# A hybrid encoder trunk on one core: half of branch C's gated product stays in on-chip memory, and the residual loads are queued behind the merge's loads

## The chip, the core and the metric

The kernel runs on one core of a Trainium2 chip. The metric is the device time of one execution, in microseconds (us). Five engines work side by side, each with its own queue of instructions that it starts in order: TensorE (PE, matmuls and transposes; its weight loads are listed as PEld), VectorE (DVE), ScalarE (ACT), GpSimd (POOL) and SyncE (SP). Here SP issues the loads of weights, and POOL issues most of the transfers of intermediate results. All transfers share 16 DMA engines. Tiles live in on-chip memory (SBUF) of 128 partitions; matmul results live in eight PSUM banks.

## The reference

The trunk has two layers over 512 positions of width 1024. Cut to what matters here:

```python
z = rms_norm(x, ln1[l]) @ w_in[l]
...
y_a = rms_norm(o_a, a_norm[l]) * silu(a_g)        # branch A: gated linear recurrence
y_b = spatial_gating(gelu(b_u), gelu(b_v), ...)   # branch B: gMLP
y_c = window_attention(qh, kh, vh, sink[l])       # branch C: windowed attention
gates = sigmoid(gz.reshape(bsz, s_len, 3, D_MODEL))
merged = (gates[:, :, 0] * (y_a @ w_br[l, 0])
          + gates[:, :, 1] * (y_b @ w_br[l, 1])
          + gates[:, :, 2] * (y_c @ w_br[l, 2]))
x = x + merged @ w_out[l]
x = x + square(relu(rms_norm(x, ln2[l]) @ w_up[l])) @ w_down[l]
```

All of it is in float32. The output is the final RMSNorm of x, 512 x 1024.

## The kernel before, in words

**Matmuls.** Each float32 product is made of three matmuls. An operand is split into a rounded high part and the rest: for weights ACT casts `wh <- wr` (L207) and DVE subtracts `wl <- wr,wh` (L208); for data the same is done at L262 and L263. A chunk of weights is 128 x 1024 (512 KB), loaded by SP (L187) into one of two raw buffers; there are three pairs of split buffers, so the cast for a later chunk waits until PE has let go of an earlier pair.

**The order of the work.** The program is written as one long sequence. A planner then simulates it with a model of its own of how long everything takes, and fixes the order on every engine's queue: an instruction that is ready in that simulation goes first, by priority. The order is therefore fixed before the kernel runs, and each engine keeps to it. Lines under `hp()` have raised priority. Semaphores and the reuse of buffers are handled by the same system, so a transfer into a buffer waits until the last reader of that buffer has finished.

**The merge of a layer.** Data is in feature order in some places and in token order in others. `proj_tok` (L254 to L256) computes a token-ordered product: four PSUM banks, one for each block of 128 tokens, 512 columns, so that a width of 1024 takes two halves (`fl` = 0 and 1). There are two groups of four banks; `proj_tok` is given one of them. The steps, for each layer, are these:

1. Branch B's gated product in feature order, `mg`, is stored to DRAM (`mgd`, L902) early.
2. The gates of branches C and A, in token order, have been stored to DRAM (`thd`) and are loaded back by `gates` (L1006) as tiles `th`.
3. Branch C: for each half, `gates`, `proj_tok` (tile `yC`), then for each token block `th <- th,yC` on DVE (L1053), a store of it to `mcd` by POOL (L1054).
4. The branch pool (`br`) ends, and the pool `Y2` (tags `yi`, `th`, `mg`) takes over its memory.
5. Branch A, for each half: `gates` (four loads `th`), four loads `mC <- mcd` (L1087), `proj_tok` (tile `yA`), then for each token block `th <- th,yA` (L1092) and the sum `mC <- mC,th` (L1093).
6. `turn_sum(fl)`: for each of four feature blocks, PE transposes the four sums into a bank (tile `mT`, L1072), POOL loads branch B's part, `mB <- mgd` (L1075), DVE adds, `mB <- mB,mT` (L1077), and the result is split into `mgh` and `mgl` (L262, L263). `turn_sum(0)` stands behind the first half in the program and uses two banks of the group that the first half has used. `turn_sum(1)` is called in the middle of the first half of the output projection.
7. The residual stream is loaded, eight tiles `xr` (L1102), from the input in layer 0 and from `xspill` in layer 1. The output projection `wo` (two halves of `proj_tok`, over eight feature blocks) follows, its first half in the banks that `turn_sum(0)` has used, and `xr <- wo,xr` (L1108) adds the residual.
8. A norm, transposes and the MLP (`up`, `dA`, `dB`, `dC`) follow.

A tile comes from `T(tag, name)`; a tag has a number of slots of 128 x 512 float32 (256 KB), listed in `SLOTS`. A tag named in `HOME` belongs to a pool that lives for a part of the layer; any other tag is permanent. The lines around step 5 are:

```python
for fl in range(2):
    th = gates("th", 1, fl)
    mc = []
    for t in range(4):
        m = T("mg", "mC")
        nc.gpsimd.dma_start(m, mcd[:, fl * 4 + t])
        mc.append(m)
    pts = proj_tok(ys, "yA", (l, "y", 0, fl), fl)
```

Of the kernel before, what the change touches and what calls it, by code (L numbers as in the profile page):

```python
# [6 lines left out]
F32 = mybir.dt.float32  # L7
# [3 lines left out]
ALU = mybir.AluOpType  # L11

P = 128
S = 512
# [46 lines left out]
def trunk(tc, xT, xt, ws, vec, fnb, bsb, snk, wst, rope, cmask, amask, ident, out):  # L61
    nc = tc.nc
# [3 lines left out]
    def pool(**kw):  # L66
        p = tc.tile_pool(**kw)
        pools.append(p)
        return p.__enter__()
# [6 lines left out]
    dram = pool(name="dram", bufs=1, space=bass.MemoryType.DRAM)  # L76

    SLOTS = {"x": 16, "l": 8, "l2": 4, "tv": 8, "rb": 1, "jk": 1,  # L80
             "xs": 16, "zt": 6,
             "yh": 8,
             "q": 2, "a": 3, "g": 2, "ch": 10,
             "yi": 16, "th": 8, "mg": 8,
             "h": 22}

    HOME = {t: p for p, ts in {"G": ("xs", "zt"), "Y1": ("yh",), "br": ("q", "a", "g", "ch"), "Y2": ("yi", "th", "mg"), "mlp": ("h",)}.items() for t in ts}
# [5 lines left out]
    def nm(s):  # L93
        ctr[0] += 1
        return f"{s}_{ctr[0]}"

    def T(tag, name, dt=F32):
        where = part[HOME[tag]] if tag in HOME else sb
        return where.tile([P, S], dt, tag=tag, bufs=SLOTS[tag], name=nm(name))

# [32 lines left out]
    def hp():  # L133

        return tc.high_priority() if boost[0] else contextlib.nullcontext()
# [104 lines left out]
    def proj_tok(xs, name, key, group, mid=None):  # L240

        pts = [PT(tag, name) for tag in GROUPS[group]]
        nk = len(xs)
        for i in range(nk // 2):
            if mid and i == nk // 4:
                mid()
            hi, lo = wload(*key, i)
            for k2 in range(2):
                k = 2 * i + k2
                c = slice(k2 * S, (k2 + 1) * S)  # L250
                for t in range(4):
                    tt = slice(t * P, (t + 1) * P)
                    xh, xl = xs[k][0][:, tt], xs[k][1][:, tt]
                    nc.tensor.matmul(pts[t], xh, hi[:, c], start=k == 0, stop=False)  # L254
                    nc.tensor.matmul(pts[t], xl, hi[:, c], start=False, stop=False)
                    nc.tensor.matmul(pts[t], xh, lo[:, c], start=False, stop=k == nk - 1)  # L256
        return pts

    def split(src, hi, lo, scale=None):

        if scale is None:
            nc.scalar.copy(hi, src)  # L262
            nc.vector.tensor_tensor(lo, src, hi.bitcast(F32), ALU.subtract)  # L263
        else:
            nc.scalar.activation(hi, src, AF.Copy, scale=scale)
            nc.vector.scalar_tensor_tensor(lo, src, scale, hi.bitcast(F32), ALU.mult, ALU.subtract)  # L266
# [39 lines left out]
    def norm_tok(which, l, xr, keep):  # L306

        n = Norm()
        n.xs, n.xf = [None] * KT, [None] * KT
        n.ss = SM("ss8", 8)  # L310

        def add(t, fl):
            j = T("jk", "jk")
            nc.scalar.activation(j, xr[t][fl], AF.Square, accum_out=n.ss[:, t * 2 + fl:t * 2 + fl + 1])

        def turn(fl, ts, bank="s"):

            w = len(ts) * P
            c0 = ts[0] * P
            for d in range(4 * fl, 4 * fl + 4):  # L320
                if n.xs[d] is None:
                    n.xs[d] = (T("x", "xh", F32R), T("x", "xl", F32R))
                    if keep:
                        n.xf[d] = Z() if d < 4 else T("l", "xf")
                pt = PT(bank, "xT")
                for i, t in enumerate(ts):
                    nc.tensor.transpose(pt[:, i * P:(i + 1) * P], xr[t][fl][:, (d % 4) * P:(d % 4 + 1) * P], id_t)
                src = pt[:, 0:w]
                parts = [x[:, c0:c0 + w] for x in n.xs[d]]
                if keep:  # L330
                    xf = n.xf[d][:, c0:c0 + w]
                    nc.scalar.activation(xf, src, AF.Copy, scale=ln_ap(which, l, d))
                    split(xf, *parts)
                else:
                    split(src, *parts, ln_ap(which, l, d))

        def end():
            s = SM("s4", 4)
            nc.vector.tensor_tensor(s, ap_of(n.ss, 0, [[2, 4]]), ap_of(n.ss, 1, [[2, 4]]), ALU.add)
            n.rc = rstd_c(s, D)  # L340

        n.add, n.turn, n.end = add, turn, end
        return n
# [345 lines left out]
    for i in range(8):  # L689
        t = T("tv", "xt")  # L690
# [5 lines left out]
    xsrc = xt  # L696
    xspill = dram.tile([P, 4, D], F32, name="xspill")
    thd = dram.tile([P, 8, D], F32, name="thd")
    mgd = dram.tile([P, KT, S], F32, name="mgd")
    mcd = dram.tile([P, 8, S], F32, name="mcd")  # L700

    for l in range(DEPTH):
        xs = n1.xs
# [176 lines left out]
        def y_split(ys, tag):  # L880
            res = []
            for y in ys:
                hi, lo = T(tag, "yh", F32R), T(tag, "yl", F32R)
                split(y, hi, lo)
                res.append((hi, lo))
            return res
# [19 lines left out]
        def gate_a():  # L906
            z = evac(proj(xs, "ag", l, "ag", len(sg)), "l2", "ag")
            th = T("jk", "th")
            nc.scalar.activation(th, z, AF.Tanh, scale=0.5)
            nc.vector.scalar_tensor_tensor(z, th, 1.0, z, ALU.add, ALU.mult)  # L910
            sg.append(z)
# [89 lines left out]
        def gates(tag, i, fl):  # L1001

            res = []
            for t in range(4):
                z = T(tag, "th")
                nc.gpsimd.dma_start(z, thd[:, i * 4 + t, fl * S:(fl + 1) * S])  # L1006
                res.append(z)
            return res
# [34 lines left out]
        with later(30000):  # L1043
            for h in range(4):
                gate_a()

            ys = y_split(yc, "yh")
            for fl in range(2):
                th = gates("ch", 0, fl)
                pts = proj_tok(ys, "yC", (l, "y", 2, fl), 0)  # L1050
                for t in range(4):
                    with hp():
                        nc.vector.scalar_tensor_tensor(th[t], th[t], 1.0, pts[t], ALU.add, ALU.mult)  # L1053
                    nc.gpsimd.dma_start(mcd[:, fl * 4 + t], th[t])  # L1054
        ys = []
        for h in range(4):
            nc.vector.scalar_tensor_tensor(oa[h], oa[h], 0.5, sg[h], ALU.mult, ALU.mult)
# [9 lines left out]
        def turn_sum(fl):  # L1067

            for d in range(4 * fl, 4 * fl + 4):
                pt = PT("s" if fl else "c", "mT")  # L1070
                for t in range(4):
                    nc.tensor.transpose(pt[:, t * P:(t + 1) * P], mcs[fl][t][:, (d % 4) * P:(d % 4 + 1) * P], id_t)  # L1072
                hi, lo = T("yi", "mgh", F32R), T("yi", "mgl", F32R)
                m = T("th", "mB")
                nc.gpsimd.dma_start(m, mgd[:, d])  # L1075
                with hp():
                    nc.vector.tensor_tensor(m, m, pt, ALU.add)  # L1077
                    split(m, hi, lo)
                ms[d] = (hi, lo)

        ms = [None] * KT
        for fl in range(2):
            th = gates("th", 1, fl)
            mc = []
            for t in range(4):
                m = T("mg", "mC")
                nc.gpsimd.dma_start(m, mcd[:, fl * 4 + t])  # L1087
                mc.append(m)
            pts = proj_tok(ys, "yA", (l, "y", 0, fl), fl)
            for t in range(4):  # L1090
                with hp():
                    nc.vector.scalar_tensor_tensor(th[t], th[t], 1.0, pts[t], ALU.add, ALU.mult)  # L1092
                    nc.vector.tensor_tensor(mc[t], mc[t], th[t], ALU.add)  # L1093
            mcs.append(mc)
            if fl == 0:
                turn_sum(0)


        xr = [[T("l", "xr"), T("l", "xr")] for _ in range(4)]
        for fl in range(2):  # L1100
            for t in range(4):
                nc.gpsimd.dma_start(xr[t][fl], xsrc[:, t, fl * S:(fl + 1) * S])  # L1102
        n2 = norm_tok("ln2", l, xr, False)
        for fl in range(2):
            pts = proj_tok(ms, "wo", (l, "wo", fl), fl, None if fl else lambda: turn_sum(1))
# [88 lines left out]
        xsrc = xspill  # L1194
# [121 lines left out]
```

## Time and profile before

| | |
|---|---|
| median of three runs | 1730.86 us (1730.69 to 1731.39) |
| profiled execution, span | 1729.5 us |
| mean granted TensorE clock | 0.996 |
| busy: PE, PEld | 97%, 81% |
| busy: DVE, ACT, POOL | 75%, 59%, 8% |
| transfers | 200.04 MB, of which POOL's queue 43.40 MB |
| stores to `mcd`, loads from it | 16 and 16, of 256 KB each |
| loads `xr` | 8 in each layer, of 256 KB each |
| merge of layer 0, of layer 1 | about 455 to 506 us, about 1313 to 1364 us |

The profile is one execution on the chip. Rows of a timeline give the start, the duration, the engine, the line of the kernel, the operation, the tile written and the tiles read, the count of merged instructions, and in brackets the idle time of the engine before it with what ended that idle time. Matmuls are pipelined, so the time that one costs is read from start to start. "Busy" of PE counts pipelined matmuls, and is an average over stages with different limits.

### The profile page before, as it was taken

How to read it: one execution, taken by the hardware profiler on the slowest of the kernel's cores; microseconds unless marked ns; L12 is line 12 of the kernel's file. 1: busy time of each engine (PE TensorE's matmuls, PEld its weight loads, DVE VectorE, ACT ScalarE, POOL GpSimd, SP SyncE). 2: the span in 40 equal slices, each digit the busy share in tenths (PEclk: the TensorE clock that was granted, in tenths of full speed). 3: DMA queues.
4: the chain of work that ended last, by engine and by line, in shares of the span. 5: the costliest groups of instructions: out<-in, count | busy, mean ns of one | idle time of the engine just before them, and what ended most of it. 6: DMA issues, size and time to landing. Idle time of an engine off the chain costs nothing.

```text
span 1729.5 us, 21976 instructions
## 1 busy us (share of the span) xinstructions
PE 1685.3 (97%) x8024; PEld 1405.0 (81%) x8024; DVE 1297.1 (75%) x2009; ACT 1017.1 (59%) x1715; POOL 146.1 (8%) x215
## 2 busy tenths in 40 slices
PE   8999999999999999999999999999999999999997
PEld 7888878887877888888888787888877878888886
DVE  7996977687566668686889869876776567686867
ACT  7665567677335555545665754877772355545454
POOL 0011200000310000000010112000004000000001
PEclk9999999999999999999999999999999999999999
DMA  8342232231545332233423422322317353232311
GB/s 331 98 146 92 83 104 81 72 104 55 203 187 182 98 110 98 98 98 98 134 92 126 147 93 71 104 79 75 111 48 273 130 182 98 98 98 97 119 65 49
DMA packets 58283, 200.04 MB, mean 116 GB/s; under 512 B 7904, under 2 KB 8288, under 8 KB 58176
## 3 DMA queue, kind: packets, MB, share of 16 engines
q1 hardware_dynamic: 44640, 154.72, 26.6%
q0 software_dynamic: 13248, 43.40, 6.7%
q8 instruction: 63, 1.03, 0.3%
q10 hardware_dynamic: 288, 0.52, 0.1%
q14 instruction: 44, 0.36, 0.1%
HBM read 177.64 MB, written 20.97 MB: 115 GB/s over the span
## 4 chain that ended last, share of the span: by engine, by line
PE 43%; issue 20%; DVE 4%; ACT 2%; POOL 0%; POOLq 0%; ACTq 0%; DVEq 0%
PE up L213 3%; PE up L212 3%; PE up L214 3%; PE dA L418 2%; PE dA L420 2%; PE dA L419 2%; PE at L558 1%; PE gA L418 1%; PE gz L214 1%; PE gz L213 1%; PE gz L212 1%; PE dC L418 1%; PE dC L420 1%; PE dC L419 1%; PE gA L420 1%
## 5 line engine op out<-in xcount | busy, mean ns | idle before, releaser
L207 ACT CAST wh<-wq 128x1024 fp32r<-128x1024 f32 x201 | 211.4, 1052 | 208.2 <-PE up L213 49.3
L208 DVE TENSOR_TENSOR wl<-wq,wh 128x1024 fp32r<-128x1024 f32 x201 | 245.1, 1222 | 117.1 <-ACT wh L207 116.1
L208 DVE TENSOR_TENSOR wl<-wr,wh 128x1024 fp32r<-128x1024 f32 x166 | 203.9, 1228 | 148.0 <-ACT wh L207 147.6
L207 ACT CAST wh<-wr 128x1024 fp32r<-128x1024 f32 x166 | 174.0, 1049 | 214.6 <-PE up L213 67.3
L212 PE MATMUL up<-xh,wh 128*128 128x512 f32 x512 | 199.2, 390 | 1.9 <-ACT u L1171 1.9
L213 PE MATMUL up<-xl,wh 128*128 128x512 f32 x512 | 200.6, 392 | 0.1
L214 PE MATMUL up<-xh,wl 128*128 128x512 f32 x512 | 199.1, 391 | 0.0
L212 PEld LDWEIGHTS up<-xh,wh 128*128 128x128 f32 x512 | 96.3, 188 | 22.7 <-ACT u L1171 2.7
L213 PEld LDWEIGHTS up<-xl,wh 128*128 128x128 f32 x512 | 96.4, 188 | 20.3 <-DVE xl L266 0.6
L214 PEld LDWEIGHTS up<-xh,wl 128*128 128x128 f32 x512 | 96.5, 189 | 19.8
L418 PE MATMUL dA<-wh,sh 128*128 128x512 f32 x256 | 99.8, 390 | 0.0
L419 PE MATMUL dA<-wh,sh 128*128 128x512 f32 x256 | 99.7, 389 | 0.0
L420 PE MATMUL dA<-wl,sh 128*128 128x512 f32 x256 | 92.6, 390 | 0.0
L600 DVE TENSOR_TENSOR ex<-ex 128x512 f32<-128x512 f32 x112 | 78.1, 715 | 6.3 <-ACT kt L575 5.4
L558 PEld LDWEIGHTS at<-qt,kt 128*128 128x128 f32 x448 | 57.0, 191 | 9.9 <-ACT kt L575 4.7
L558 PE MATMUL at<-qt,kt 128*128 128x128 f32 x448 | 59.6, 276 | 5.6 <-DVE qt L573 2.7
L572 ACT ACTIVATE qt<-ex 128x512 f32<-128x512 f32 x56 | 37.7, 674 | 46.3 <-DVE ex L600 38.5
L274 POOL TENSOR_TENSOR rs<-ms,mhalf_t 128x4 f32<-128x4 f32 (+2 forms) x15 | 17.3, 1156 | 530.6 <-DVE ms L272 527.5
L420 PEld LDWEIGHTS dA<-wl,sh 128*128 128x128 f32 x256 | 48.1, 188 | 10.0
L418 PEld LDWEIGHTS dA<-wh,sh 128*128 128x128 f32 x256 | 48.1, 188 | 10.0
L419 PEld LDWEIGHTS dA<-wh,sh 128*128 128x128 f32 x256 | 48.1, 188 | 9.9
L262 ACT CAST sh<-sf 128x512 fp32r<-128x512 f32 x64 | 39.7, 621 | 24.3 <-DVE sf L383 18.0
(403 smaller groups left out, 4403.0 us busy)
## 6 DMA issues: line engine op xcount, KB each, us to landing
wr<-in_ws_dram SPq DMA_DIRECT2D x166, 512.0 KB, 3.3
wq<-in_ws_dram SPq DMA_DIRECT2D x117, 512.0 KB, 4.3
thd<-zt POOLq DMA_DIRECT2D x32, 256.0 KB, 2.5
th<-thd POOLq DMA_DIRECT2D x32, 256.0 KB, 4.6
mgd<-mg POOLq DMA_DIRECT2D x16, 256.0 KB, 2.9
mcd<-th POOLq DMA_DIRECT2D x16, 256.0 KB, 2.5
mC<-mcd POOLq DMA_DIRECT2D x16, 256.0 KB, 6.7
mB<-mgd POOLq DMA_DIRECT2D x16, 256.0 KB, 6.6
```

Source lines behind the costliest of these rows:

```text
L207: nc.scalar.copy(hi, raw)
L208: nc.vector.tensor_tensor(lo, raw, hi.bitcast(F32), ALU.subtract)
L212: nc.tensor.matmul(pt, whi, xhi, start=first, stop=False)
L213: nc.tensor.matmul(pt, whi, xlo, start=False, stop=False)
L214: nc.tensor.matmul(pt, wlo, xhi, start=False, stop=last)
L262: nc.scalar.copy(hi, src)
L418: nc.tensor.matmul(pt, xh[:, t], hi[:, c], start=start and k == 0, stop=False, skip_group_check=True)
L419: nc.tensor.matmul(pt, xl[:, t], hi[:, c], start=False, stop=False, skip_group_check=True)
L420: nc.tensor.matmul(pt, xh[:, t], lo[:, c], start=False, stop=k == 3, skip_group_check=True)
L558: nc.tensor.matmul(pt[:, c], kk(st), qq[:, c], start=True, stop=True)
L572: nc.scalar.activation(qt.rearrange(shp, b=nb, h=2), e_q, AF.Exp)
L600: nc.vector.tensor_tensor(o_ap, o_ap, ap_of(ex, i_, [[istep, 2]] + z), ALU.add)
```

## The change

Branch C's gated product of the first half (`fl` = 0) is written into four permanent tiles (tag `mk`) and stays there; it is no longer stored to `mcd` and loaded back. The sum at L1093 then works in place on these tiles. The second half is stored and loaded as before. The slots of `mg` go from eight to four, and `mcd` to half its size. Each of the eight `xr` loads gets an order edge on POOL's queue: it is issued behind the last load `mC <- mcd` of the second half. The scratch memory for POOL's DMA descriptors is set to 4096 bytes, where it had its default.

```diff
-             "yi": 16, "th": 8, "mg": 8,
+             "yi": 16, "th": 8, "mg": 4,
...
+    SLOTS = {"x": 16, "l": 8, "l2": 4, "mk": 4, "tv": 8, "rb": 1, "jk": 1,
...
-    mcd = dram.tile([P, 8, S], F32, name="mcd")
+    mcd = dram.tile([P, 4, S], F32, name="mcd")
...
+            kept = []
             for fl in range(2):
                 th = gates("ch", 0, fl)
                 pts = proj_tok(ys, "yC", (l, "y", 2, fl), 0)
                 for t in range(4):
+                    if fl == 0:
+                        kept.append(T("mk", "mC"))
+                    m = th[t] if fl else kept[t]
                     with hp():
-                        nc.vector.scalar_tensor_tensor(th[t], th[t], 1.0, pts[t], ALU.add, ALU.mult)
-                    nc.gpsimd.dma_start(mcd[:, fl * 4 + t], th[t])
+                        nc.vector.scalar_tensor_tensor(m, th[t], 1.0, pts[t], ALU.add, ALU.mult)
+                    if fl:
+                        nc.gpsimd.dma_start(mcd[:, t], m)
...
-            mc = []
-            for t in range(4):
-                m = T("mg", "mC")
-                nc.gpsimd.dma_start(m, mcd[:, fl * 4 + t])
-                mc.append(m)
+            mc = kept if fl == 0 else [T("mg", "mC") for _ in range(4)]
+            if fl:
+                for t in range(4):
+                    ld = nc.gpsimd.dma_start(mc[t], mcd[:, t])
...
-                nc.gpsimd.dma_start(xr[t][fl], xsrc[:, t, fl * S:(fl + 1) * S])
+                with tc.issue_after(ld.ins):
+                    nc.gpsimd.dma_start(xr[t][fl], xsrc[:, t, fl * S:(fl + 1) * S])
...
-    nc = _bacc.Bacc("TRN2", target_bir_lowering=False, num_devices=1)
+    nc = _bacc.Bacc("TRN2", target_bir_lowering=False, num_devices=1, dynamic_dma_scratch_size=4096)
```

More of the change, by code (lines that the diff above doesn't have):

```diff
@@ L76, in trunk @@
     dram = pool(name="dram", bufs=1, space=bass.MemoryType.DRAM)
-    SLOTS = {"x": 16, "l": 8, "l2": 4, "tv": 8, "rb": 1, "jk": 1,
+    SLOTS = {"x": 16, "l": 8, "l2": 4, "mk": 4, "tv": 8, "rb": 1, "jk": 1,
              "xs": 16, "zt": 6,
```

## The prediction

> **What bounds the kernel now.** I read the page first, for the bound, and its list of DMA issues, for the transfers that the change touches.
>
> ```profile
> span 1729.5 us, 21976 instructions
> PE 1685.3 (97%) x8024; PEld 1405.0 (81%) x8024; DVE 1297.1 (75%) x2009; ACT 1017.1 (59%) x1715; POOL 146.1 (8%) x215
> ...
> mcd<-th POOLq DMA_DIRECT2D x16, 256.0 KB, 2.5
> mC<-mcd POOLq DMA_DIRECT2D x16, 256.0 KB, 6.7
> ```
>
> TensorE (PE) is busy for 97% of the span, and the change gives it not one matmul less. So the change can only win what PE loses by waiting around the merge, and can only lose by making PE wait more. POOL, which issues the transfers, is busy for 8%: the issues themselves are worth nothing. The profiled execution has a span of 1729.5 us and the runs a median of 1730.86 us; I work in the span and add the 1.4 us between them. A measurement of this kernel can tell about 0.2% (3.46 us) from no change.
>
> Next, the busy time by stretches of 8 us through layer 0's merge. Columns: PE, PEld, DVE, ACT, POOL busy, granted clock, DMA share, GB/s.
>
> ```profile
> 472.00:480.00 8.00, 7.33 (x39) 5.56 (x38) 5.47 (x8) 3.32 (x4) 4.83 (x9) 1.00 1.03 419
> 480.00:488.00 8.00, 7.28 (x31) 5.74 (x31) 6.11 (x11) 2.29 (x3) 3.22 (x6) 1.00 1.03 413
> ```
>
> Here PE has holes, and the DMA engines are full (share 1.03, 413 to 419 GB/s). The timeline of PE shows where the holes are (start, duration, line, tile, count, idle before it).
>
> ```profile
> 476.59 0.39 PE L255 MATMUL yA<-wh,yl 128*128 128x512 f32 x1
> 476.82 0.40 PE L256 MATMUL yA<-wl,yh 128*128 128x512 f32 x1
> 477.06 0.60 PE L1072 MATMUL mT<-id_t,mC 128*128 128x128 f32 x4
> 478.33 1.26 PE L1072 MATMUL mT<-id_t,mC 128*128 128x128 f32 x8 [0.67 <-DVE mB L1077]
> 479.34 0.70 PE L254 MATMUL wo<-wh,mgh 128*128 128x512 f32 x2
> 480.66 0.50 PE L254 MATMUL wo<-wh,mgh 128*128 128x512 f32 x1 [0.62 <-DVE mB L1077]
> 481.26 0.50 PE L255 MATMUL wo<-wh,mgl 128*128 128x512 f32 x1
> ...
> 491.64 1.03 PE L1072 MATMUL mT<-id_t,mC 128*128 128x128 f32 x8
> ```
>
> Matmuls overlap, so I count from start to start. A 512-column matmul takes 0.23 us of queue (476.59 to 476.82), a transpose 0.126 (478.33 to 479.34 for eight). Four transposes from 477.06 should have ended 0.50 later, and the next row comes 1.27 later: 0.77 lost. Two matmuls from 479.34 need 0.46 and take 1.32: 0.86 lost. One from 480.66 needs 0.23 and takes 0.60: 0.37 lost. Sum 2.00 us in layer 0. The chain of waits, which covers layer 1's merge, shows the same place there:
>
> ```profile
> 1335.27 0.34 PE mT L1072 x3
> 1335.78 0.39 issue
> 1336.24 0.68 DVE mB L1077
> 1337.11 0.86 issue
> 1337.97 0.68 DVE mB L1077
> 1338.65 0.61 DVE mgl L263
> 1339.31 0.51 PE wo L255
> ```
>
> From 1335.61 to 1339.31 (3.70 us) the path runs over VectorE (DVE): sum, add of branch B, split. PE does eight transposes and three matmuls meanwhile, 1.70 us, so it loses 2.00 again. Both layers: **4.0 us is what the change can take from this stall**.
>
> **The change part by part.** Why the first half's sums are late stands in DVE's timeline of layer 0, with the ScalarE (ACT) row behind one entry.
>
> ```profile
> 466.88 1.29 DVE L1092 SCALAR_TENSOR_TENSOR th<-th,yA 128x512 f32<-128x512 f32 x2 [1.79 <-DMA th<-thd]
> ...
> 469.32 1.28 DVE L1092 SCALAR_TENSOR_TENSOR th<-th,yA 128x512 f32<-128x512 f32 x2
> 470.51 0.69 DVE L1093 TENSOR_TENSOR mC<-mC,th 128x512 f32<-128x512 f32 x1
> 471.93 0.69 DVE L1093 TENSOR_TENSOR mC<-mC,th 128x512 f32<-128x512 f32 x1 [0.73 <-DMA mC<-mcd]
> 474.27 1.23 DVE L208 TENSOR_TENSOR wl<-wr,wh 128x1024 fp32r<-128x1024 f32 x1 [1.65 <-ACT wh L207]
> 475.41 1.29 DVE L1093 TENSOR_TENSOR mC<-mC,th 128x512 f32<-128x512 f32 x2
> 477.58 1.29 DVE L1077 TENSOR_TENSOR mB<-mB,mT 128x512 f32<-128x512 f32 x2 [0.88 <-PE mT L1072]
> ```
> ```profile
> 473.18 1.05 ACT L207 CAST wh<-wr 128x1024 fp32r<-128x1024 f32 x1 [5.04 <-DMA wr<-in_ws_dram]
> ```
>
> The four gated products of branch A are done at 470.6 (469.32 + 1.28). The sums with C's products then come at 470.51, at 471.93 (0.73 late, its load), and two at 475.41, behind a weight split that waits for ACT, which waited 5.04 us for a weight load. The last sum ends at 476.70, and all mT, B's adds and the first output projection follow from it. The order on DVE is written by a planner that simulates the program; it put the weight split ahead of sums whose operand it thought not yet loaded.
>
> *Kept half.* Per layer four stores and four loads of 256 KB go, 2.1 MB in all. The multiply writes another tile of the same shape, so DVE does nothing more. The sums for the first half then wait only for branch A's product. Two rows above start their second instruction 0.60 after their first (1.29 for two that overlap), so four sums after 470.6 end at 473.0 instead of 476.70: 3.7 us earlier, against a hole of 2.00 us.
>
> *What is late next.* DVE still has, before the first output projection can run, four adds of B (2.4 us at that pitch), one weight split (1.2) and two of mgl's splits (1.2): from 473.0 this ends at 477.8, and about 479.1 if each add waits for its transposes. PE, without holes, would start that projection at 477.06 + 12 × 0.126 = 478.6, and needs the first mgl three matmuls later, at 479.3. So DVE is in time, by 0.2 to 1.5 us, and I take all 2.00 us as gone. B's operand mB has to be there too, which POOL's timeline and two landing times decide:
>
> ```profile
> 457.96 1.60 POOL L1102 DMA_DIRECT2D xr<-in_xt_dram  x3
> ...
> 462.13 2.12 POOL L1006 DMA_DIRECT2D th<-thd  x4 [1.82 <-DMA mcd<-th]
> ...
> 466.98 2.43 POOL L1075 DMA_DIRECT2D mB<-mgd  x4
> ...
> 477.37 1.17 POOL L1006 DMA_DIRECT2D th<-thd  x2
> ...
> 480.04 0.54 POOL L1006 DMA_DIRECT2D th<-thd  x1 [0.26 <-DVE wl L208]
> ```
> ```profile
> DMA to landing us min/median/max: 5.7/7.1/8.6
> ```
> ```profile
> DMA to landing us min/median/max: 4.6/5.3/7.2
> ```
>
> The first landing line is of the mB loads, the second of the th loads, both in layer 0's merge. Today four xr and four mC loads are issued ahead of mB. Without them mB can follow th directly, at 462.13 + 2.12 = 464.25, and its first tile lands at 471.4 by the median. If the planner puts the second half's four mC loads first (0.54 each), it is 473.5, still about when the sums end.
>
> The Trainium skill's page "DMA: Bandwidth & Descriptors", in Anatomy of one DMA, speaks against the change: a POOL-issued transfer costs about 2.0 us plus its bytes at 436 GB/s. As an estimate that is 2.6 us for 256 KB, so the removed loads would have been hidden already. The row here (6.7 us to land) disagrees, in a stretch where the engines are full; the measurement decides, and the case has its chance below.
>
> *Residual loads behind the merge's.* The edge moves the four xr loads of 457.96 from ahead of th to behind the second half's last mC load, and keeps the other four behind it as well. Their user is the residual add after the projection, 20 us later, so they may wait. Queued behind them on POOL can be the second half's th and mB loads. Taken out ahead of th: up to 4 × 256 KB of traffic, 2.5 us at 413 GB/s. The th load waited 1.82 us for a mcd store to land and DVE 1.79 us for th, so the front can move by 0 to 1.8 us. I take 0, since the store still stands in front, and keep 1.8 us as more slack.
>
> *Slots and scratch.* Slots for mC go from eight to four, and four are used; the kept tiles are rewritten one layer later. The DMA scratch is made smaller. No row shows its filling. It cannot gain; if it held fewer transfers in flight, the loads of the merge would come one landing (5.3 to 7.1 us) later. POOL's rows show only issues of 0.54 us and waits for named transfers, so I take 0.
>
> Sum: 1729.5 − 2 × 2.00 = 1725.5 of span, + 1.4 = **1726.9 us**.
>
> **The rivals.**
>
> *The order stays.* The planner may still place the weight split ahead of the last two sums, since it is the planner's clock and not the chip's that decides. Then the sums end when the weight lands. For it: the place is the same in both layers' holes. Against: the split was there because the operand was not. Even so, 1 MB of mC loads less ahead of that weight is up to 2.5 us at 413 GB/s, so each layer keeps between 0 and 2.0 us of its stall. I take 0.5 won per layer: 1729.9 us.
>
> *The loads were hidden anyway.* If only 0.73 us of a sum really waited for a load, and the holes come from adds, splits and bank turns in series, mT moves and the holes stay: 1730.9 us. The chain above, which is DVE throughout, speaks for it; the sums' 3.7 us speaks against it.
>
> *The stall moves to the second half, and grows.* The second half's sums end now at the moment when PE transposes them (491.64), with no hole. Two of DVE's rows there:
>
> ```profile
> 487.30 1.23 DVE L208 TENSOR_TENSOR wl<-wr,wh 128x1024 fp32r<-128x1024 f32 x1 [1.89 <-ACT wh L207]
> ...
> 490.24 1.29 DVE L1093 TENSOR_TENSOR mC<-mC,th 128x512 f32<-128x512 f32 x2
> ```
>
> They end at 491.53. If PE arrives 2.0 us earlier, at 489.6, they must too. The 1.89 us that DVE idles there says that they can, if th is there: the last th is issued at 480.04 and lands at 485.3 by the median. But if all eight xr loads go in front of those th loads, 2.1 MB at 413 GB/s is 5.1 us: landing at 492.3 with the maximum of 7.2, sums at 493.6, and PE waits 4.0 us at 489.6. Net 2.0 us lost per layer: 1734.9 us. It decides from sums later than 491.6 (no gain) and 493.4 (slower by over 0.2%). Against it: th's slots come free 3.7 us earlier, and POOL has little before them.
>
> **How the numbers follow.** Forecast 0.50, order stays 0.26, hidden anyway 0.13, moved stall 0.11. In the forecast case PE may still lose the third hole (0.37 per layer, 1727.6), or gain a little more from the earlier th, which I bound at 0.65 per layer (a third of the stall again, an estimate): 1725.6. The high end has to take in "order stays" and "hidden" with the runs' own spread (1730.69 to 1731.39): 1731.5. Left out is the moved stall. Most of the forecast case and some of "order stays" lies beyond 3.46 us: faster 0.47. The rest of those with "hidden": same 0.42. Slower 0.11.
>
> **What would show it.** Right: no mT row with idle before it from mB, and the first wo following the last yA or mT without a hole; the four first-half sums directly behind their L1092, ending about 473; PE busy 8.00 in the stretches that show 7.33 and 7.28; DMA total lower by 4.2 MB; every xr load behind the second half's mC loads. Wrong: L208 still between the sums (order stays); sums early but holes of the same size (hidden); idle PE ahead of the second group of mT and DVE waiting for th there (moved stall); or a changed order outside the merge, which this argument holds to be none.

## The result, and the profile after

The changed kernel takes 1724.37 us (median of five runs, 1721.52 to 1725.66), the kernel before 1730.86 us (1726.91 to 1731.42, five runs). The ratio is 0.9963, with a 95% interval of 0.9951 to 0.9975: faster, by 4.3 to 8.5 us. The forecast was 1726.9 us within 1725.6 to 1731.5; the time lies 1.2 us below that range. The page of the changed kernel:

```profile
span 1720.8 us, 21948 instructions
PE 1680.9 (98%) x8024; PEld 1403.0 (82%) x8024; DVE 1297.3 (75%) x2009; ACT 1016.7 (59%) x1715; POOL 137.4 (8%) x199
...
q0 software_dynamic: 11968, 39.20, 6.2%
```

PE does the same 8024 matmuls, and POOL's queue moves 4.2 MB less (39.20 against 43.40). The same two stretches of the first merge, by engine (PE, PEld, DVE, ACT, POOL, clock, DMA share, GB/s):

```profile
472.00:480.00 8.00, 8.00 (x45) 6.67 (x44) 6.04 (x9) 4.04 (x6) 5.37 (x10) 1.00 1.03 414
480.00:488.00 8.00, 8.00 (x37) 6.64 (x36) 7.82 (x12) 1.34 (x2) 2.69 (x5) 1.00 1.02 407
```

PE has no idle time left in them, and the DMA engines are as full as before (share 1.03 and 1.02). What changed is not that the memory traffic got light. PE's timeline there (line numbers are five higher than before):

```profile
471.32 0.27 PE L1077 MATMUL mT<-id_t,mC 128*128 128x128 f32 x1
...
476.57 0.39 PE L256 MATMUL yA<-wl,yh 128*128 128x512 f32 x1
476.80 1.03 PE L1077 MATMUL mT<-id_t,mC 128*128 128x128 f32 x8
477.59 0.71 PE L254 MATMUL wo<-wh,mgh 128*128 128x512 f32 x2
478.14 0.40 PE L255 MATMUL wo<-wh,mgl 128*128 128x512 f32 x1
...
488.59 1.03 PE L1077 MATMUL mT<-id_t,mC 128*128 128x128 f32 x8
```

The transposes mT begin at 471.32, inside branch A's second half. The eight that stand behind it, and the output projection wo, follow without a bracket: no idle time. In the kernel before, the first transposes stood near the end of that half:

```profile
475.68 0.38 PE L1072 MATMUL mT<-id_t,mC 128*128 128x128 f32 x2
475.82 0.48 PE L256 MATMUL yA<-wl,yh 128*128 128x512 f32 x1
476.14 0.38 PE L1072 MATMUL mT<-id_t,mC 128*128 128x128 f32 x2
```

None of these rows has a bracket either: PE did not wait for a sum there. This matters below. DVE and POOL of the changed kernel:

```profile
464.63 1.28 DVE L1096 SCALAR_TENSOR_TENSOR th<-th,yA 128x512 f32<-128x512 f32 x2 [0.28 <-PE yA L256]
465.83 0.69 DVE L1097 TENSOR_TENSOR mC<-mC,th 128x512 f32<-128x512 f32 x1
467.27 0.69 DVE L1096 SCALAR_TENSOR_TENSOR th<-th,yA 128x512 f32<-128x512 f32 x1 [0.76 <-DMA th<-thd]
467.88 0.68 DVE L1097 TENSOR_TENSOR mC<-mC,th 128x512 f32<-128x512 f32 x1
469.27 0.69 DVE L1096 SCALAR_TENSOR_TENSOR th<-th,yA 128x512 f32<-128x512 f32 x1 [0.71 <-DMA th<-thd]
469.88 0.68 DVE L1097 TENSOR_TENSOR mC<-mC,th 128x512 f32<-128x512 f32 x1
470.48 1.22 DVE L208 TENSOR_TENSOR wl<-wr,wh 128x1024 fp32r<-128x1024 f32 x1
471.62 0.68 DVE L1097 TENSOR_TENSOR mC<-mC,th 128x512 f32<-128x512 f32 x1
...
474.83 1.28 DVE L1082 TENSOR_TENSOR mB<-mB,mT 128x512 f32<-128x512 f32 x2 [0.56 <-DMA xr<-in_xt_dram]
```
```profile
461.52 2.13 POOL L1006 DMA_DIRECT2D th<-thd  x4 [4.29 <-DMA mcd<-th]
463.64 2.12 POOL L1080 DMA_DIRECT2D mB<-mgd  x4
465.76 1.06 POOL L1092 DMA_DIRECT2D mC<-mcd  x2
...
470.76 0.54 POOL L1107 DMA_DIRECT2D xr<-in_xt_dram  x1 [0.76 <-DMA mB<-mgd]
```

The first three sums follow their gated products at once; what paces them now is the products' own `th` loads (0.76 and 0.71 us of waiting). The last sum ends at 472.30 (471.62 + 0.68), against 476.70 before, although a weight split still stands ahead of it. On POOL mB comes right behind th, and all residual loads stand behind the second half's four mC loads. (The bracket at 474.83 names a residual load that landed then; the add does not use it. The transposes that it adds had just been made, at 474.52.)

**A measure without the noise.** The runs of the kernel before spread over 4.5 us, as much as the effect. So I use a stretch of the trace: from the first yA matmul to the first up matmul. Before it is 80.41 us in layer 0 (448.17 to 528.58) and 80.43 in layer 1; after 77.79 (447.43 to 525.22) and 77.83. Each layer gains 2.6 us, **5.2 us together**, 0.30% of the time. The two profiled spans differ by 8.7 us; the other 3.5 us lie outside the merge. About 1.7 of them is a phase of half clock that this one execution of the kernel before had (the last section), and about 0.7 stands already ahead of the first yA. The rest, about 1 us, is not traced.

### The profile page after: what moved, and what is told of

The parts are those of the page before. It is cut to its first block, busy times and chain, and to the rows that moved or that the text cites. A ratio compares the mean times of both kernels' runs of the same rounds, so it can differ in the third digit from the quotient of the medians.

```text
span 1720.8 us, 21948 instructions
## 1 busy us (share of the span) xinstructions
PE 1680.9 (98%) x8024; PEld 1403.0 (82%) x8024; DVE 1297.3 (75%) x2009; ACT 1016.7 (59%) x1715; POOL 137.4 (8%) x199
## 3 DMA queue, kind: packets, MB, share of 16 engines
q1 hardware_dynamic: 44640, 154.72, 26.6%
q0 software_dynamic: 11968, 39.20, 6.2%
q8 instruction: 63, 1.03, 0.2%
## 4 chain that ended last, share of the span: by engine, by line
PE 40%; issue 22%; DVE 4%; ACT 2%; POOL 1%; DMA 0%; POOLq 0%; ACTq 0%; DVEq 0%
PE up L213 3%; PE up L212 3%; PE up L214 3%; PE dA L418 2%; PE dA L420 2%; PE dA L419 2%; PE at L558 1%; PE gz L213 1%; PE gz L214 1%; PE gz L212 1%; PE dC L418 1%; PE dC L420 1%; PE dC L419 1%; PE wo L254 1%; PE wo L255 1%
```

## The experiments

Each ratio is against runs of the kernel before on the same chip. Stretch: first yA to first up. "Sums end": end of the last sum of the first and of the second half, after the first yA, in layer 0 / layer 1.

| kernel | ratio (95% interval) | stretch | first half's sums end | second half's |
|---|---|---|---|---|
| before | | 80.41 / 80.43 | 28.5 / 28.3 | 43.4 / 43.4 |
| changed | 0.9963 (0.9951 to 0.9975) | 77.79 / 77.83 | 24.9 / 24.0 | 40.5 / 40.1 |
| n0 before again | 0.9998 (0.9989 to 1.0007) | 80.39 / 80.40 | 27.8 / 28.0 | 43.3 / 43.3 |
| e1 kept half, no edge | 0.9964 (0.9951 to 0.9977) | 77.79 / 77.74 | 26.1 / 24.8 | 40.7 / 40.2 |
| e2 edge only | 0.9997 (0.9988 to 1.0005) | 80.45 / 79.60 | 27.0 / 25.1 | 45.0 / 44.2 |
| e4 kept half, dead traffic | 0.9972 (0.9964 to 0.9981) | 78.27 / 78.31 | 23.2 / 23.2 | 42.3 / 42.3 |
| e5 keep six tiles | 0.9960 (0.9948 to 0.9972) | 77.81 / 77.77 | 23.7 / 23.2 | 40.1 / 39.6 |
| e6 keep the second half | 0.9966 (0.9954 to 0.9977) | 77.76 / 77.76 | 23.8 / 23.3 | 39.6 / 39.6 |
| e9 the same, no edge | 0.9961 (0.9948 to 0.9973) | 77.81 / 77.76 | 23.4 / 23.7 | 39.6 / 39.6 |
| e3 scratch only | 0.9987 (0.9978 to 0.9997) | 80.41 / 80.36 | 26.9 / 28.3 | 43.4 / 43.3 |
| e3b the same again | 0.9988 (0.9979 to 0.9997) | 80.41 / 80.39 | 27.2 / 27.8 | 43.4 / 43.3 |
| e10 changed, scratch 8192 | 0.9964 (0.9952 to 0.9977) | 77.85 / 77.81 | 23.8 / 23.2 | 40.2 / 40.0 |
| e7 changed, weight sums later | 0.9923 (0.9910 to 0.9936) | 77.82 / 77.82 | 23.2 / 23.2 | 40.3 / 40.0 |
| e8 before, weight sums later | 0.9956 (0.9944 to 0.9969) | 80.45 / 80.40 | 27.6 / 27.8 | 43.4 / 43.4 |

**The kept half without the edge (e1).**

```diff
-                with tc.issue_after(ld.ins):
-                    nc.gpsimd.dma_start(xr[t][fl], xsrc[:, t, fl * S:(fl + 1) * S])
+                nc.gpsimd.dma_start(xr[t][fl], xsrc[:, t, fl * S:(fl + 1) * S])
```

> The changed kernel without the order edge: the first half of branch C's product stays on the chip, and the residual loads may again be issued ahead of the merge's loads. Theory (the sums no longer wait for a load, so the planner puts the transposes into branch A's second half): PE's three holes at the first half's transposes (2.0 us per layer before, none after the change) stay gone or shrink to under 0.5 us per layer; time 1724 to 1727 us, within 2 us of the changed kernel. Rival 1 (the edge carries the gain, by taking 1 MB of residual loads out of the way): holes of 1.5 to 2.0 us per layer are back and the time is 1729 to 1731 us.

1724.95 us, and the whole gain of the stretch. Four residual loads do go ahead of th again, and the first half's sums end 1.2 us later than in the changed kernel in layer 0; nobody waits for that. The edge is not needed for the gain.

**The edge alone (e2).** In the kernel before, with `ld` the last of the eight `mC` loads:

```diff
-                nc.gpsimd.dma_start(m, mcd[:, fl * 4 + t])
+                ld = nc.gpsimd.dma_start(m, mcd[:, fl * 4 + t])
...
+                with tc.issue_after(ld.ins):
+                    nc.gpsimd.dma_start(xr[t][fl], xsrc[:, t, fl * S:(fl + 1) * S])
```

> The kernel before with the order edge alone: both halves are stored and loaded as before, and all eight residual loads are issued behind the last of the eight loads of branch C's product. Theory: the sums still wait for their loads, which land up to 2.5 us earlier because 1 MB is out of the way; the holes shrink from 2.0 to 0.5 to 2.0 us per layer; time 1728 to 1731 us. Rival 1 (the edge carries the gain): no holes, 1724 to 1726 us.

1729.59 us, no gain; but not for the reason that I gave. The holes at the first half are gone: there is no idle time of PE from the first yA to the second half's transposes. DVE waits 2.35 us for a load and still ends these sums at 474.26:

```profile
470.03 0.69 DVE L1093 TENSOR_TENSOR mC<-mC,th 128x512 f32<-128x512 f32 x1 [2.35 <-DMA mC<-mcd]
...
472.37 1.89 DVE L1093 TENSOR_TENSOR mC<-mC,th 128x512 f32<-128x512 f32 x3
...
491.60 0.69 DVE L1093 TENSOR_TENSOR mC<-mC,th 128x512 f32<-128x512 f32 x1
```

The last row is the second half's last sum: it ends at 492.29, 45.0 after the first yA (43.4 before). PE and POOL there:

```profile
488.20 0.39 PE L256 MATMUL wo<-wl,mgh 128*128 128x512 f32 x1
489.27 0.44 PE L1072 MATMUL mT<-id_t,mC 128*128 128x128 f32 x2 [0.69 <-DVE th L1092]
...
494.74 0.66 PE L1072 MATMUL mT<-id_t,mC 128*128 128x128 f32 x4 [0.67 <-DVE mB L1077]
```
```profile
473.53 1.80 POOL L1103 DMA_DIRECT2D xr<-in_xt_dram  x3
...
476.30 0.54 POOL L1006 DMA_DIRECT2D th<-thd  x1
...
481.39 0.54 POOL L1006 DMA_DIRECT2D th<-thd  x1 [0.69 <-DVE wl L208]
```

The residual loads now stand among the second half's th loads, the last of which is issued 34.1 us after the first yA (31.9 before, 30.9 in the changed kernel), and the holes have moved to the second half. Here PE does wait, for a product (0.69 us) and for a sum (0.29 us, at 490.00). This is the mechanism of my rival "the stall moves to the second half", in a kernel that has the edge without the four removed loads: it eats the gain in layer 0, and all but 0.8 us of it in layer 1, and does not go beyond it.

**The kept half, with the traffic put back (e4).** The first half is kept, and is also stored and loaded into tiles that nobody reads, so that this kernel moves 4.2 MB more than it needs (the slots of `mg` and the size of `mcd` are those of before):

```diff
-                    if fl:
-                        nc.gpsimd.dma_start(mcd[:, t], m)
+                    nc.gpsimd.dma_start(mcd[:, fl * 4 + t], m)
...
-            if fl:
-                for t in range(4):
-                    ld = nc.gpsimd.dma_start(mc[t], mcd[:, t])
+            for t in range(4):
+                ld = nc.gpsimd.dma_start(mc[t] if fl else T("mg", "mU"), mcd[:, fl * 4 + t])
```

> The changed kernel with the traffic put back and nothing waiting for it: the first half is kept on the chip, and is also stored to DRAM and loaded into tiles that nobody reads; these loads are queued on POOL where the kernel before had them. It does the reference's work and 4.2 MB of transfers more than needed. Theory (what counts is that the sums do not wait for a load): holes of under 0.7 us per layer, time 1724 to 1727 us. Rival 3 (the gain is 4.2 MB less traffic in a stretch where the DMA engines are full): holes of 1.5 to 2.0 us per layer, time 1729 to 1731 us.

```profile
462.28 2.12 POOL L1090 DMA_DIRECT2D mU<-mcd  x4 [0.17 <-issue]
464.39 1.06 POOL L1079 DMA_DIRECT2D mB<-mgd  x2
```

The dead loads (mU) stand ahead of mB as the real ones did. The stretch is 78.3 us: 2.13 of the 2.62 us per layer remain. So four fifths of the gain is there although the loads are still made: what counts is that no sum depends on them. The other 0.5 us per layer is one hole, in both layers:

```profile
487.89 0.60 PE L1076 MATMUL mT<-id_t,mC 128*128 128x128 f32 x4
489.00 0.50 PE L254 MATMUL wo<-wh,mgh 128*128 128x512 f32 x1 [0.51 <-ACT wh L207]
```

The second half's sums end at 42.3, and only four transposes stand here in PE's order (eight in the changed kernel, at 488.59), so that PE runs out of work while ACT casts the next weights. The extra loads thus cost through the second half's order; whether by their bytes or by their places in POOL's queue is not separated.

**Six tiles kept (e5).**

```diff
-                    if fl == 0:
-                        kept.append(T("mk", "mC"))
-                    m = th[t] if fl else kept[t]
+                    far = fl and t > 1
+                    if not far:
+                        kept.append(T("mk", "mC"))
+                    m = th[t] if far else kept[fl * 4 + t]
...
```

> The changed kernel with six of the eight product tiles kept on the chip (all of the first half and two of the second), 2.1 MB less traffic than the changed kernel over both layers. Theory (only the first half's sums stand on PE's path): stretch from the first yA to the first up stays at 77.8 us per layer within 0.3, time within 0.1% of the changed kernel (1723 to 1726 us). Rival 3 (less traffic is the gain): another 1.3 us per layer, 1721 to 1722 us.

The stretch does not move (77.81 and 77.77). With no hole left in it, less traffic buys nothing there.

**The other half kept (e6, e9).** The condition is turned round: `kept` holds the second half, and the first is stored and loaded. e6 has the edge, e9 has not.

```diff
-                    if fl == 0:
+                    if fl == 1:
                         kept.append(T("mk", "mC"))
-                    m = th[t] if fl else kept[t]
+                    m = kept[t] if fl else th[t]
...
```

> The second half is kept on the chip and the first half is stored and loaded: the same 4.2 MB less traffic as the changed kernel, but in the half whose sums PE did not wait for; the residual loads are ordered behind the first half's loads. Theory (the first half's sums are what counts): holes at the first half's transposes of 1 to 2 us per layer, stretch of 79 to 80.4 us, time 1727 to 1730 us. Rival 3 (traffic): stretch of 77.8 us, 1724 to 1726 us. If the edge alone moved the stall to the second half's sums for want of their loads, then keeping the second half together with the edge also ends at 77.8 us, and both halves' operands have to be early: this is the theory's other outcome, told from rival 3 by the timeline (no wait of DVE for a load in the second half).

> The second half kept on the chip, the first half stored and loaded, and no order edge: four residual loads may again be issued ahead of the merge's loads. Two explanations of why keeping the second half gained as much as keeping the first: (a) the first half's loads were late only because residual loads and a late store stood ahead of them on POOL's queue; then without the edge they are 1.5 to 2.5 us later again and the holes come back at least in part, stretch 78.5 to 80.4 us per layer; (b) fewer loads alone are enough, wherever the residual loads stand; then the stretch stays at 77.8 us within 0.3.

Both give the full gain, 77.8 us. So my theory in its narrow form, that the first half has to be kept because its sums are the late ones, falls. POOL's rows of e6 show that the first half's loads come earlier:

```profile
457.63 2.20 POOL L1006 DMA_DIRECT2D th<-thd  x4 [8.94 <-DVE on L1062]
459.82 2.12 POOL L1092 DMA_DIRECT2D mC<-mcd  x4
```

The last product of branch C is no longer stored, so th does not wait for that store (461.52 in the changed kernel, 457.63 here), and the first half's loads are issued at 459.82 instead of 464.24 and later. In e9 the planner put the residual loads behind mB without being told to. So e9 does not tell whether residual loads ahead of th would have hurt there; (a) and (b) of its expectation are not separated.

**The scratch, and the comparison with itself (e3, e3b, n0, e10).**

```diff
-    nc = _bacc.Bacc("TRN2", target_bir_lowering=False, num_devices=1)
+    nc = _bacc.Bacc("TRN2", target_bir_lowering=False, num_devices=1, dynamic_dma_scratch_size=4096)
```

> The kernel before with the DMA scratch set to 4096 bytes alone. Theory and rival 1: same order, same holes of 2.0 us per layer, time within 0.1% of before (1729 to 1732 us). Rival 2 (the smaller scratch changes how many transfers of POOL's queue are in flight): POOL's waits for landings change and the time moves by more than 2 us either way.

> The kernel before with the DMA scratch at 4096 bytes, a second time: the first comparison gave a ratio of 0.9987 (0.9978 to 0.9997) although the order of the instructions on every engine and the merge's stretch are those of before. Theory (chance): within 0.0010 of 1. Rival 2 (the scratch saves time outside the merge): 0.9980 to 0.9992 again.

> The kernel before, unchanged, compared with itself: what the comparison shows where nothing differs. Every theory: ratio 1.000, and its distance from 1 is the size of what such a comparison can show by chance; at most 0.001.

> The changed kernel with twice the DMA scratch (8192 bytes), the same order of instructions on every engine. Theory: stretch of 77.8 us, ratio to before 0.9950 to 0.9975 as the changed kernel. Rival 2 (the small scratch is part of the gain): ratio 0.0008 or more above the changed kernel's 0.9963.

With the scratch alone the order of PE, DVE, ACT and POOL is that of before, and the stretch is too. Yet the ratio came out at 0.9987 and 0.9988, with intervals that end at 0.9997, while the kernel before against itself gave 0.9998 (0.9989 to 1.0007). If 0.1% is real, it lies outside the merge; the size of the scratch does not show (0.9964 with 8192 in the changed kernel). I cannot name a cause. It stays open. No run has the changed kernel with the default scratch, so the 1.3 us of the measured 6.5 that the merge does not explain may belong to it.

**A version that beats both (e7, e8).** In the changed kernel PE's largest hole nearby is behind the merge, where the MLP begins:

```profile
531.55 0.63 PE L212 MATMUL up<-xh,wh 128*128 128x512 f32 x2
534.16 0.66 PE L327 MATMUL xT<-id_t,xr 128*128 128x128 f32 x4 [1.98 <-DVE xl L266]
```
```profile
532.22 1.23 DVE L403 TENSOR_TENSOR wq<-wq,wq 128x1024 f32<-128x1024 f32 x1 [2.33 <-DMA wq<-in_ws_dram]
533.36 1.40 DVE L266 SCALAR_TENSOR_TENSOR xl<-xT,vec_t,xh 128x512 fp32r<-128x512 f32 x2
```

A sum of weights (L403) waits 2.33 us for its load at the head of DVE's queue, and the split that PE needs (L266) stands behind it. One edge turns this round (`n2.last` is the last of those splits; the lines that hand it over are left out):

```diff
                 if f == 4:
-                    early_sums(raw)
+                    with tc.issue_after(n2.last.ins):
+                        early_sums(raw)
```

> The changed kernel with one more order edge: in each group of the MLP, DVE's sums of down-projection weights are queued behind the last split of the transposed residual, since in the profile a sum that waits for its weight load stands ahead of that split and PE loses 1.8 to 2.7 us per layer there. Theory (an instruction that waits for a load stands ahead of others on DVE, as in the merge): that hole falls below 0.5 us per layer, time 1719 to 1722 us. Rival (the split itself or the transposes are late anyway): the hole stays above 1.5 us and the time within 0.1% of the changed kernel.

> The kernel before with only the order edge of the last run: in the MLP, DVE's sums of down-projection weights behind the last split of the transposed residual; the merge is as before. Theory: the two holes are independent; the stretch from the first yA to the first up stays at 80.4 us per layer, the hole at the transposed residual (1.8 to 2.7 us per layer) goes, and the time is 0.9955 to 0.9975 of before. Rival (the two edits work through the same wait): less than 2 us gained, ratio above 0.9988.

The rows of e7:

```profile
531.22 1.41 DVE L266 SCALAR_TENSOR_TENSOR xl<-xT,vec_t,xh 128x512 fp32r<-128x512 f32 x2 [1.23 <-ACT xh L265]
...
535.97 2.35 DVE L403 TENSOR_TENSOR wq<-wq,wq 128x1024 f32<-128x1024 f32 x2
```

The split comes 2.1 us earlier, the hole is gone in both layers, and e7 takes 1717.1 us, the fastest version here. On the kernel before, the same edge alone gives 0.9956 with the merge's stretch unchanged. The two edits add up: 0.9963 x 0.9956 is 0.9919, and 0.9923 was measured.

## Where the prediction was wrong, and what it had right

*The bound and the place: right.* PE was bound, and the gain is PE's holes around the first half's transposes. They are gone, and the signs named for it came: three of the four sums directly behind their products, PE busy for 8.00 of 8.00, 4.2 MB less, every residual load behind the second half's mC loads.

*The term that failed: "2.00 us" per layer.* It measured 2.62 us. I counted three holes from PE's rows and stopped there. By the marks of the trace in layer 0: from the first yA to the first wo 31.17 became 30.16 (1.01; I had 0.77 for the first hole, and the eight transposes behind it also cost less once they directly follow a running matmul). From there to the second half's first mT 12.30 became 11.00 (1.30; I had 0.86 + 0.37 = 1.23). From there to the first up 36.94 became 36.63 (0.31; I had nothing). In that last part the kernel before lost 0.2 us at a matmul of wo that waited for a weight split, which had waited 1.21 us for ACT's cast; the changed kernel has four transposes and four other matmuls in that place, and does not wait. Two marks and the same 367 matmuls and transposes between them hold all of it at once; three holes read by eye did not.

*The low end of the range: wrong.* It was set at 1.3 us below the forecast, on a guess about one more hole, and took in nothing of the spread of the measurement. I had three runs (1730.69 to 1731.39) and took their 0.04% for the noise; later runs of the same kernel lay between 1726.61 and 1734.38. With the right term the forecast would have been 1725.7, next to the range's end of 1725.6. The measured 6.5 us is another 1.3 above what the two stretches explain, well within its own interval (4.3 to 8.5); whether that is spread or the scratch stays open.

*The step from late sums to PE's holes: wrong, and the holes went for another reason.* I wrote that the last sum ends at 476.70 and that all mT, B's adds and the first output projection follow from it. But in the kernel before PE waits for no sum of the first half: the first transposes run at 475.68, and those at 477.06 directly behind the last yA. Five profiles have this order of PE (before, n0, e3, e3b, e8). In their ten merges these sums end anywhere from 26.9 to 28.5 us after the first yA, and the holes are the same every time: 0.67 us, then 0.60 to 0.62, stretch 80.36 to 80.45. In e2 they end at 27.0 in layer 0, inside that span, and the holes are not there.

What differs is PE's fixed order. How many yA matmuls stand behind the first and behind the eighth transpose:

| kernels | behind the first | behind the eighth | first mT, after the first yA | holes behind it |
|---|---|---|---|---|
| before, n0, e3, e3b, e8 | 4 | 0 | 27.5 to 27.6 | 0.67 and 0.6 us |
| e2 | 19 | 9 | 24.1 | none |
| e1 | 8 | 6 | 26.6 | none |
| changed, e4 to e7, e9, e10 | 20 | 9 | 23.9 | none |

Eight transposes fill the two banks, and B's adds must empty these before the next eight. Before, PE had no other work left meanwhile; with six or more yA matmuls behind the eighth, it has. So the change worked because the planner, with no load ahead of the first half's sums, put the transposes earlier. My sum left them where they were; in that order sums that are 1.6 us earlier (e3) gained nothing. That the forecast was near is therefore in part luck. Why the planner put them late before, that it held the loads for later than they were, is argued: its own times are not on record.

*Right for too narrow a reason.* I held that the first half's own loads were the point. e6 shows that keeping the second half does as well, e2 that the edge alone also removes the first holes, and moves them. There, and only there, PE's brackets name a late product or sum: those of e2's second half end at 45.0 and 44.2, and PE reaches its transposes at 42.0 and 41.2. With sums that end by 40.7, in all kernels that have the full gain, there is no hole. Before, the order had the first half's holes, and the edge alone the second half's. Four loads taken off the sums' path, those of either half, avoided both.

*The sum's end and DVE's slack.* "Four sums after 470.6 end at 473.0" came out as 472.30, since the products themselves were ready sooner. "A first mB tile at 471.4" fits: its load was issued at 463.64 (forecast 464.25) and landed 6.8 us later, and the adds ran from 474.83.

*"The order stays" and "hidden anyway".* Neither happened. The first rival was right that the planner's order decides, but looked at DVE's: a split still stands ahead of the last sum, and nothing waits for that.

*The price for a transfer.* By the 2.6 us estimated from the Trainium skill's page "DMA: Bandwidth & Descriptors", Anatomy of one DMA, the removed loads would have been hidden. In layer 0's merge of the kernel before the mC loads took 5.3 to 8.3 us to land, and e4 shows that taking them off the sums' path was worth 2.1 us per layer.

## What to carry to other kernels

Where a planner fixes the order, a load can cost through the place that its readers are given, and not only through the time at which it lands: compare the order of the bounding engine before and after, and see whether it really waits for the late tile. Where transfers share one queue that is full, ask for each of them when its reader is due, and take off the path those that can stay on the chip; here, moving others behind them without removing any only moved the stall to the next due time (e2). An instruction that waits for a load at the head of an in-order queue delays everything behind it: look for it in the brackets, then put it behind what the bounding engine needs (in e8 one order edge gained as much as the whole change). Price such a stall by the distance between two marks on the bounding engine, not by the holes that stand out.

## What the hardware showed besides

POOL's queue had room for eight transfers. In none of the 14 profiles are more than eight in flight: no issue starts before the one eight places ahead of it has landed, and in the merge, once the queue is full, most start 0.28 to 0.57 us after that landing. In the changed kernel the mC load at 469.47 stands eight behind the th load of 463.12, which landed at 469.18. So a transfer put ahead of others costs them a place as well as bytes. Whether the hardware or the program's own semaphores set the eight is not shown.

PE's holes can cost more than their length. The kernel before, layer 1, around the hole at the transposed residual (clock in the third column from the end):

```profile
1393.00:1395.00 2.00, 0.59 (x3) 0.16 (x1) 0.98 (x1) 0.08 (x1) 0.00 (x0) 1.00 1.02 410
1395.00:1397.00 2.00, 1.04 (x7) 0.97 (x8) 2.00 (x4) 0.35 (x1) 0.00 (x0) 1.00 1.02 418
1397.00:1400.00 3.00, 3.00 (x11) 2.46 (x10) 3.00 (x4) 0.86 (x2) 0.00 (x0) 0.53 1.01 414
1400.00:1403.00 3.00, 3.00 (x13) 2.41 (x12) 1.28 (x2) 0.16 (x1) 0.00 (x0) 0.90 0.08 31
```

After a hole of 2.54 us (counted from start to start, 0.17 more than the bracket in PE's row) the granted clock falls to half for 3.4 us: 0.47 x 3 + 0.10 x 3 = 1.7 us lost. Over the twelve profiles that have this hole, once in each layer, none of the nine holes of up to 2.16 us was followed by such a phase, and 11 of the 15 from 2.25 to 2.77 us were. The length of one hole does not decide alone: near 1080, in all 14 profiles, two brackets of 1.6 and 2.0 us come 3 us apart, and a phase of lower clock shows there every time. In e7 and e8, without the hole, there is none at this place. This is one part of the spread between executions of one kernel, and probably of e7's and e8's gain beyond the holes themselves (argued, not measured apart). The Trainium skill's page "TensorE: Matmul & The Clock Gate", in Part 1, says that the array goes to half rate after an idle window of about 3.4 us; here single holes from 2.25 us were enough, in 11 of 15 cases.
